# A row-sum kernel: the last two rows loaded in column pieces and shared by two engines, and the group stores moved from the POOL queue to the ACT queue

## The chip, the cores and the metric

The kernel runs on one core of one Trainium2 chip. The metric is the device time of one execution in microseconds (us), read on the chip. The profile of the kernel before is of a run that took 163.31 us.

Three words are used throughout. A load or store is *issued* when a queue (SP, ACT or POOL) hands it to the 16 DMA engines; it has *landed* when its semaphore is complete in the trace; its *packets* are the trace's records of what the DMA engines moved. The engines are VectorE (DVE in the profile), ScalarE (ACT), GpSimd (POOL) and SyncE (SP).

## The reference

```python
def setup_inputs():
    batch, seq, dim = 32, 512, 1024
    return {"x": np.random.randn(batch, seq, dim).astype(np.float32)}

def reference(x):
    return np.sum(x, axis=-1).astype(np.float32)
```

The kernel reads 67.11 MB, adds up 16384 rows of 1024 numbers, and writes 64 KB. There is next to nothing to compute; the loads set the time.

## The kernel before

Each of the 128 partitions gets 128 rows, in 8 groups of 16. Groups 0 to 6 are one 8 MB load each, into three rotating buffers. VectorE adds up all 16 rows of a tile in one instruction; in the seventh tile ScalarE takes half of the rows, with the accumulator of an ACTIVATE whose ordinary output nobody reads. The eighth group is loaded in shrinking parts (8, 4, 2, 1 rows), and its last row in three column pieces, so that little work is left when the last bytes arrive.

```python
        def vec(dst, src):
            nc.vector.tensor_reduce(
                out=dst, in_=src, axis=mybir.AxisListType.X, op=mybir.AluOpType.add
            )

        def act(dst, src, n):
            nc.scalar.activation(
                out=scratch[:, :n],                  # one SBUF tile, not read by anyone
                in_=src,
                func=mybir.ActivationFunctionType.Copy,
                accum_out=dst,
            )
        # ... rows_of(): one load, then vec() on the first rows and act() on the others
        def store(eng, g0, g1):
            eng.dma_start(
                out=out_v[:, g0:g1],
                in_=sums[:, g0 * BIG : g1 * BIG].rearrange("p (g j) -> p g j", j=BIG),
            )

        for i in range(nbig):                        # seven 8 MB tiles
            t = inpool.tile([P, BIG * dim + 2], fp32)
            rows_of(t, 0, BIG, i * BIG, BIG // 2 if i == nbig - 1 else 0)
            if i % 3 == 2:
                store(nc.gpsimd, i - 2, i + 1)       # group stores, POOL queue
        store(nc.gpsimd, nbig - 1, nbig)
        # ... parts of 8, 4 and 2 rows, shared by both engines; one whole row for ScalarE
        cuts = [0, 384, 768, dim]                    # the last row
        for c0, c1 in zip(cuts, cuts[1:]):
            nc.sync.dma_start(out=last[:, c0:c1], in_=rows_from(j, 1)[:, 0, c0:c1])
        for i, (c0, c1) in enumerate(zip(cuts, cuts[1:])):
            if c1 < dim:
                vec(last[:, dim + i : dim + i + 1], last[:, c0:c1])   # partial sums, beside the data
            else:
                vec(sums[:, j : j + 1], last[:, c0 : dim + i])        # 256 columns + 2 partial sums
        store(nc.sync, nbig, nbig + 1)
```

## Time and profile before

| | before |
|---|---|
| time, median of 3 runs | 162.79 us (162.73 to 162.85) |
| span of the profile | 161.5 us |
| load packets | 1.0 to 157.90 us |
| last piece landed | 158.37 us |
| last reduction | 158.68 to 159.10 us |
| final store | issued 159.17, landed 160.59 us |

First the page of the kernel before: busy time of each engine, the DMA line of the table by slices (tenths of busy time, 40 slices), the load queue with its share of 16 engines' span, and the chain that ended last by line.

```profile
span 161.5 us, 124 instructions
...
DVE 121.4 (75%) x13; ACT 19.7 (12%) x33; POOL 2.4 (1%) x7
...
DMA  8997998997997997996996996996997996999990
...
q1 hardware_dynamic: 2160, 67.12, 97.1%
...
DMA t<-in_x_dram 74%; DVE sums L66 22%; SPq L81 1%; DVE t L66 1%; DVEq L66 0%
```

The load queue fills 97.1% of the span and VectorE 75%, so the DMA stream is the bound. The 22% of VectorE in the chain is the time in which a later load waits in the queue for its buffer; the stream does not run dry meanwhile, because two more loads are under way. A steady 64 KB packet takes 2.418 us in the trace, so 16 engines move 16 x 65536 B / 2.418 us = 433.7 GB/s. The Trainium skill, "DMA: Bandwidth & Descriptors", Where 436 GB/s comes from, puts the ceiling of the ports at 435.2 GB/s, and the trace agrees. In the middle of this kernel next to nothing can be gained.

The end is another matter. This is the timeline of the kernel before (start, duration, engine, line, instruction; in brackets how long the engine sat idle before it and for what):

```profile
138.55 8.69 DVE L66 TENSOR_REDUCE sums<-t 128x8 f32<-128x8192 f32 x1 [2.15 <-DMA t<-in_x_dram]
...
157.09 1.06 ACT L71 ACTIVATE scratch<-t 128x1024 f32<-128x1024 f32 x1
157.64 1.01 DVE L66 TENSOR_REDUCE t<-t 128x1 f32<-128x384 f32 x2 [0.68 <-DMA t<-in_x_dram]
158.06 0.19 ACT L71 ACTIVATION_READ_ACCUMULATOR scratch<-t 128x1 f32 x1
158.68 0.42 DVE L66 TENSOR_REDUCE sums<-t 128x1 f32<-128x258 f32 x1
159.17 0.35 SPq L88 DMA_DIRECT2D out_dram<-sums  x1
```

The last piece has landed at 158.37, but VectorE is still on its two 384-column pieces (the "x2" line) until 158.66. So the last reduction starts 0.31 us after its data is there, and all of the final store and the closing barriers follow it.

### The profile page before, as it was taken

The page shows a single profiled execution, that of the slowest core. Times are in us where ns is not written, and L with a number is a line of the kernel's source. Part 1 is how long each engine was busy: PE and PEld are TensorE (multiplying, and loading weights), DVE is VectorE, ACT ScalarE, POOL GpSimd, SP SyncE. Part 2 cuts the span into 40 slices and gives each one's busy share as a digit, 9 for nine tenths or more (in the row PEclk, how much of TensorE's full clock was granted, in tenths as well). Part 3 has the DMA queues.
Part 4 walks back from the last instruction along what each step waited for, and adds up shares of the span by engine and source line. Part 5 has one row for each costly group of instructions (what it writes and reads, how often), then busy time and mean ns, then how long its engine had stood idle before and what let it go on. Part 6 is the DMA issues. An engine that isn't in the chain of part 4 may idle for free.

```text
span 161.5 us, 124 instructions
## 1 busy us (share of the span) xinstructions
DVE 121.4 (75%) x13; ACT 19.7 (12%) x33; POOL 2.4 (1%) x7
## 2 busy tenths in 40 slices
DVE  0000049998699968999499994999949997697883
ACT  3000000000000000000000000000000000698891
POOL 0000000000000000000200000000000001001000
DMA  8997998997997997996996996996997996999990
GB/s 260 519 438 341 519 406 373 519 438 341 519 454 325 519 471 308 519 487 292 519 493 293 519 487 292 519 487 292 519 454 325 519 487 292 391 491 389 410 392 14
DMA packets 2256, 67.18 MB, mean 416 GB/s; under 512 B 416, under 2 KB 848, under 8 KB 976
## 3 DMA queue, kind: packets, MB, share of 16 engines
q1 hardware_dynamic: 2160, 67.12, 97.1%
q0 software_dynamic: 96, 0.06, 0.1%
HBM read 67.11 MB, written 0.07 MB: 416 GB/s over the span
## 4 chain that ended last, share of the span: by engine, by line
DMA 74%; DVE 22%; SPq 1%; issue 0%; DVEq 0%
DMA t<-in_x_dram 74%; DVE sums L66 22%; SPq L81 1%; DVE t L66 1%; DVEq L66 0%
## 5 line engine op out<-in xcount | busy, mean ns | idle before, releaser
L66 DVE TENSOR_REDUCE sums<-t 128x16 f32<-128x16384 f32 (+5 forms) x11 | 120.4, 10941 | 37.1 <-DMA t<-in_x_dram 37.0
L71 ACT ACTIVATE scratch<-t 128x1024 f32<-128x1024 f32 x16 | 16.9, 1057 | 137.8 <-DMA t<-in_x_dram 137.3
L88 POOL DMA_DIRECT2D out_dram<-sums x3 | 2.2, 732 | 146.2 <-DVE sums L66 135.4
L71 ACT ACTIVATION_READ_ACCUMULATOR scratch<-t 128x1 f32 x16 | 3.0, 186 | 0.0
L66 DVE TENSOR_REDUCE t<-t 128x1 f32<-128x384 f32 x2 | 1.0, 549 | 0.7 <-DMA t<-in_x_dram 0.7
L71 ACT ACT_TABLE_LOAD x1 | 1.3, 1283 | 0.8 <-PEq L135 0.8
L135 POOL MEMSET const-float32-0.0<- 128x1 f32 x1 | 0.1, 98 | 0.2 <-issue 0.2
L135 POOL MEMSET const-bfloat16-1.0<- 128x1 bf16 x1 | 0.1, 101 | 0.0
L135 POOL MEMSET const-uint8-127<- 128x1 uint8 x1 | 0.1, 99 | 0.0
L135 POOL MEMSET const-float32-1.0<- 128x1 f32 x1 | 0.1, 98 | 0.0
## 6 DMA issues: line engine op xcount, KB each, us to landing
t<-in_x_dram SPq DMA_DIRECT2D x1, 4096.0 KB, 31.2
t<-in_x_dram SPq DMA_DIRECT2D x1, 2048.0 KB, 35.9
t<-in_x_dram SPq DMA_DIRECT2D x1, 1024.0 KB, 37.8
t<-in_x_dram SPq DMA_DIRECT2D x1, 512.0 KB, 38.6
t<-in_x_dram SPq DMA_DIRECT2D x2, 192.0 KB, 38.6
t<-in_x_dram SPq DMA_DIRECT2D x1, 128.0 KB, 38.4
t<-in_x_dram SPq DMA_DIRECT2D x7, 40.8
out_dram<-sums POOLq DMA_DIRECT2D x2, 24.0 KB, 7.9
```

The costliest lines, as they stand in the source:

```text
L66: nc.vector.tensor_reduce(out=dst, in_=src, axis=mybir.AxisListType.X, op=mybir.AluOpType.add)
L71: nc.scalar.activation(out=scratch[:, :n], in_=src, func=mybir.ActivationFunctionType.Copy, accum_out=dst,)
L81: nc.sync.dma_start(out=block, in_=rows_from(j, n))
L88: eng.dma_start(out=out_v[:, g0:g1], in_=sums[:, g0 * BIG : g1 * BIG].rearrange("p (g j) -> p g j", j=BIG),)
L135: nc = _bacc.Bacc("TRN2", target_bir_lowering=False, num_devices=1)
```

## The change

The intent has three parts: share the last two rows between VectorE and ScalarE, so that the last reduction does not queue behind VectorE's other pieces; take the group stores out of the load stream and make one ACT-queue store of them at the end; and let ScalarE write its unread output to PSUM, with four buffers. The diff, cut (`tc.manual_schedule()` came with the change):

```diff
-        tc.tile_pool(name="scratch", bufs=1) as spool,
+        tc.tile_pool(name="unread", bufs=4, space=bass.MemoryType.PSUM) as upool,
+        tc.manual_schedule(),
 ...
-            if i % 3 == 2:
-                store(nc.gpsimd, i - 2, i + 1)
-        store(nc.gpsimd, nbig - 1, nbig)
 ...
-        rows_of(t, a, 1, nbig * BIG + a, 1)          # and the last row in 384, 384, 256
+        for width in (640, 256, 128):                # two rows in each piece
+            if len(parts) == k:
+                at += k                              # room for row 0's partial sums
+            part = t[:, at : at + 2 * width].rearrange("p (n d) -> p n d", n=2)
+            nc.sync.dma_start(out=part, in_=rows_from(j, 2)[:, :, c : c + width])
+            ...
+        for i, part in enumerate(parts[:k]):
+            vec(w[:, i : i + 1], part[:, 0, :])                       # row 0: VectorE
+            act(w[:, k + 2 * width + i : ...], part[:, 1, :], pieces[i])  # row 1: ScalarE
+        store(nc.scalar, 0, last)                    # all seven group stores at once
+        vec(sums[:, j : j + 2], w.rearrange("p (n d) -> p n d", n=2)) # 2 x (128 + 2)
         store(nc.sync, last, last + 1)
```

The partial sums of row 0 stand just ahead of the last piece and those of row 1 just behind it, so one reduction over two runs of 130 finishes both rows. The order of instructions on VectorE is unchanged; on ScalarE the store comes after its second piece.

More of the change, by code (lines that the diff above doesn't have):

```diff
@@ L51, in rows_from @@
         return x_g[j // BIG, :, j % BIG : j % BIG + n, :]
-    nbig = J // BIG - 1
-    tail = [(8, 4), (4, 2), (2, 1)]
+    last = J // BIG - 1
+    pieces = (640, 256, 128)
     with (
         tc.tile_pool(name="in", bufs=3) as inpool,
-        tc.tile_pool(name="scratch", bufs=1) as spool,
+        tc.tile_pool(name="unread", bufs=4, space=bass.MemoryType.PSUM) as upool,
         tc.tile_pool(name="stage", bufs=1) as stpool,
+        tc.manual_schedule(),
     ):
         sums = stpool.tile([P, J], fp32)
-        scratch = spool.tile([P, dim], fp32)
         def vec(dst, src):
@@ L70, in act @@
         def act(dst, src, n):
+            unread = upool.tile([P, dim], fp32)
             nc.scalar.activation(
-                out=scratch[:, :n],
+                out=unread[:, :n],
                 in_=src,
@@ L76, in act, with rows @@
             )
-        def rows_of(t, a, n, j, n_act):
+        def rows(t, a, n, j, n_act):
             nv = n - n_act
@@ L81, in rows_of @@
             nc.sync.dma_start(out=block, in_=rows_from(j, n))
-            if nv:
-                vec(sums[:, j : j + nv], block[:, :nv, :])
+            vec(sums[:, j : j + nv], block[:, :nv, :])
             for q in range(nv, n):
@@ L91, in store @@
             )
-        for i in range(nbig):
-            t = inpool.tile([P, BIG * dim + 2], fp32)
-            rows_of(t, 0, BIG, i * BIG, BIG // 2 if i == nbig - 1 else 0)
-            if i % 3 == 2:
-                store(nc.gpsimd, i - 2, i + 1)
-        store(nc.gpsimd, nbig - 1, nbig)
-        t = inpool.tile([P, BIG * dim + 2], fp32)
+        for g in range(last):
+            t = inpool.tile([P, BIG * dim + 4], fp32)
+            rows(t, 0, BIG, g * BIG, BIG // 2 if g == last - 1 else 0)
+        t = inpool.tile([P, BIG * dim + 4], fp32)
         a = 0
-        for n, n_act in tail:
-            rows_of(t, a, n, nbig * BIG + a, n_act)
+        j = last * BIG
+        for n in (8, 4, 2):
+            rows(t, a, n, j + a, n // 2)
             a += n
-        rows_of(t, a, 1, nbig * BIG + a, 1)
-        a += 1
-        j = nbig * BIG + a
-        last = t[:, a * dim :]
-        cuts = [0, 384, 768, dim]
-        for c0, c1 in zip(cuts, cuts[1:]):
-            nc.sync.dma_start(out=last[:, c0:c1], in_=rows_from(j, 1)[:, 0, c0:c1])
-        for i, (c0, c1) in enumerate(zip(cuts, cuts[1:])):
-            if c1 < dim:
-                vec(last[:, dim + i : dim + i + 1], last[:, c0:c1])
-            else:
-                vec(sums[:, j : j + 1], last[:, c0 : dim + i])
-        store(nc.sync, nbig, nbig + 1)
+        j += a
+        at = a * dim
+        k = len(pieces) - 1
+        parts = []
+        c = 0
+        for width in pieces:
+            if len(parts) == k:
+                at += k
+            part = t[:, at : at + 2 * width].rearrange("p (n d) -> p n d", n=2)
+            nc.sync.dma_start(out=part, in_=rows_from(j, 2)[:, :, c : c + width])
+            parts.append(part)
+            at += 2 * width
+            c += width
+        w = t[:, at - 2 * width - k : at + k]
+        for i, part in enumerate(parts[:k]):
+            vec(w[:, i : i + 1], part[:, 0, :])
+            act(w[:, k + 2 * width + i : k + 2 * width + i + 1], part[:, 1, :], pieces[i])
+        store(nc.scalar, 0, last)
+        vec(sums[:, j : j + 2], w.rearrange("p (n d) -> p n d", n=2))
+        store(nc.sync, last, last + 1)
 _INS = ['x']
```

## The prediction

> What bounds the kernel now. The DMA stream. The chain of waits gives 74% of the span to loads and its last 38.6 us are the load queue; the table by slices shows DMA near full until the last slice, and the queue table puts the load queue's packets at 97.1% of 16 engines' span. In the packet records, load packets run from 1.0 us to 157.90 us of a 161.5 us span. VectorE is 75% busy and ScalarE 12%: both have slack until the last two rows. So only three things can move the time: work added to or taken from the DMA stream, the stretch from last landing to the final reduction, and the stores after it.
>
> The tail before. The last piece's semaphore is complete at 158.37, but VectorE runs three short reductions in a row (384, 384, 258 elements: 0.55, 0.54, 0.42 us) and starts the last at 158.68, ending 159.10. The final store is issued at 159.17, its packets move 160.01 to 160.22, it has landed at 160.59, and 0.9 us of closing barriers follow.
>
> What the change does.
> 1. Stream, removed: three POOL stores. Their packets cost each DMA engine two 65 ns, one 27 ns and three 9 ns records, about 0.18 us, all before the stream's end.
> 2. Stream, added: the last two rows now come in runs of 2560, 1024 and 512 bytes. The records give 159 ns for 4096 B, 66 for 1536, 46 for 1024 and 27 for 512, so I estimate 103 for 2560. Per engine: 16 x (103+46.5+27) = 2.82 us against 8 x 159 + 16 x 66 + 8 x 46.5 = 2.70 us. Net about +0.1 us; with 1, the last landing moves about 0.1 us earlier, to 158.3.
> 3. Last reduction. Estimated landings 157.1, 157.85, 158.3. VectorE (about 1.05 ns an element plus 0.14 us) does 640 and 256 elements by 158.4. ScalarE takes 1057 ns for 1024 elements today; the Trainium skill, "ScalarE: Activation LUTs", What ACT_TABLE_LOAD costs, gives 0.833 ns an element, which leaves 0.2 us fixed. This trace has one length only and cannot confirm the slope. With the 0.09 us by which the accumulator read outlasts it, ScalarE finishes its two pieces near 158.6. So the last reduction (two rows of 130, 0.42 us) starts at about 158.65 and ends at 159.05: one wait, VectorE's own queue, is exchanged for another, ScalarE's. Gain 0 to 0.15 us. ScalarE's output in PSUM may take a little off each ACTIVATE.
> 4. Moved into the tail: one ACT-queue store of 896 runs of 64 B. Its wait is long satisfied, so it issues right after ScalarE's second piece is dispatched, about 158.1. At 11 ns a run (the final store's records) it costs each engine 56 x 11 = 0.6 us. If it starts 0.84 us after issue, as the final store does, it is done by about 159.9, before the final store's packets at 160. Little slack: if generating 896 runs is slower, it delays the final store or lands last.
>
> Everything before 155 us should stay as it was. Sum: 0.1 to 0.3 us gained, against a possible 0 to 1 us lost to the ACT store.
>
> Predicted 162.7 us, range 162.0 to 163.7; faster by over 2%: 2%; within 2%: 94%; slower by over 2%: 4%.
>
> Right if: the last landing is within 0.2 us of 158.3; the last VectorE reduction is released by ScalarE and ends 158.9 to 159.2; ACT-queue packets end before the final store's start. Wrong if: the ACT store's packets run past 160.1, or the final store's first packet comes later than 0.85 us after issue; or the stream ends earlier by over 0.3 us, which would mean that the POOL stores cost loads more than their own packets; or fixed launch cost outside the span changes as POOL's queue falls idle.

## The result, and the profile after

| | before | after |
|---|---|---|
| time, median of 4 runs | 162.82 us (162.73 to 163.11) | 162.98 us (162.72 to 163.11) |
| ratio | | 1.0005 (95% interval 0.9987 to 1.0022) |
| span of the profile | 161.5 us | 161.2 us |

A ratio is the mean time of one kernel's fast runs over that of the other's in the same rounds, so it is not quite the ratio of the medians.

The page of the kernel after, the same lines and the new queue q10, which is the ACT store:

```profile
span 161.2 us, 123 instructions
...
DVE 121.5 (75%) x13; ACT 18.5 (12%) x35; POOL 0.2 (0%) x4
...
DMA  8996996996996996996996996996996996998992
...
q1 hardware_dynamic: 2400, 67.12, 97.3%
q10 hardware_dynamic: 912, 0.06, 0.3%
...
DMA t<-in_x_dram 75%; DVE sums L67 22%; SPq L83 1%; DVE t L67 1%; ACTq L89 0%; ACT unread L73 0%; DVEq L67 0%
```

The timeline of the kernel after:

```profile
138.14 8.69 DVE L67 TENSOR_REDUCE sums<-t 128x8 f32<-128x8192 f32 x1 [2.32 <-DMA t<-in_x_dram]
...
157.09 1.14 DVE L67 TENSOR_REDUCE t<-t 128x1 f32<-128x640 f32 x2 [0.54 <-DMA t<-in_x_dram]
157.15 0.71 ACT L73 ACTIVATE unread<-t 128x640 f32<-128x640 f32 x1 [0.61 <-DMA t<-in_x_dram]
157.79 0.19 ACT L73 ACTIVATION_READ_ACCUMULATOR unread<-t 128x1 f32 x1
157.88 0.37 ACT L73 ACTIVATE unread<-t 128x256 f32<-128x256 f32 x1
157.94 0.41 ACTq L89 DMA_DIRECT2D out_dram<-sums  x1
158.19 0.19 ACT L73 ACTIVATION_READ_ACCUMULATOR unread<-t 128x1 f32 x1
158.41 0.42 DVE L67 TENSOR_REDUCE sums<-t 128x2 f32<-128x260 f32 x1 [0.18 <-ACT unread L73]
158.86 0.36 SPq L89 DMA_DIRECT2D out_dram<-sums  x1
```

VectorE now has a gap before the last reduction, "[0.18 <-ACT unread L73]": the wait that ends last changed its owner, as intended. But the last piece landed at 158.12, so the last reduction still starts 0.29 us after its data: VectorE is on its second piece until 158.23, 0.11 us, and then waits 0.18 us for ScalarE. The ACT store is issued under ScalarE's last ACTIVATE; its packets run from 158.90 to 159.63, and the final store's first packet follows at 159.72.

The span is 0.3 us shorter while the time is not. The two traces differ before the change has done anything: the first load landed at 22.39 before and at 21.69 after, mostly because the first round of 64 KB packets took 3.57 us on average in one profile (the slowest 3.98) and 3.11 us in the other (3.36), with the same code at the start. The whole span is therefore a poor measure of a change this small. Counting from the landing of the last 8 MB tile removes that. The table below is worked out from semaphore, instruction and packet records of each trace; it has the experiments too, which come next. "Closing" is from the final store's landing to the end of the span.

| trace | last piece landed, us after the last 8 MB tile | last reduction starts, us after that piece | it ends, us after the tile | closing, us | end of span, us after the tile |
|---|---|---|---|---|---|
| before | 19.85 | 0.31 | 20.58 | 0.95 | 23.01 |
| before_again | 19.85 | 0.32 | 20.59 | 0.94 | 23.00 |
| after | 20.00 | 0.29 | 20.72 | 0.88 | 23.05 |
| a_repeat (after) | 19.92 | 0.30 | 20.65 | 0.88 | 22.98 |
| b_pieces_pool | 20.00 | 0.30 | 20.72 | 1.01 | 23.20 |
| c_store_only | 19.77 | 0.31 | 20.50 | 0.82 | 22.80 |
| c_again | 19.85 | 0.34 | 20.60 | 0.81 | 22.89 |
| d_scratch_sbuf | 19.93 | 0.45 | 20.80 | 0.88 | 23.14 |
| f_store_early | 20.08 | 0.17 | 20.67 | 0.88 | 23.01 |
| g_no_cut | 19.68 | 0.02 | 21.99 | 1.01 | 24.51 |
| h_cut_even | 19.96 | 0.15 | 20.67 | 0.88 | 23.01 |

Two traces of the same kernel differ by 0.01 to 0.10 us in the last column, against up to 0.2 us in the span. In that column before is 23.01 and after 23.02 (means of two): no difference.

### The profile page after: what moved, and what is told of

The parts are those of the page before. It is cut to its first block, busy times and chain, and to the rows that moved or that the text cites. A ratio compares the mean times of both kernels' runs of the same rounds, so it can differ in the third digit from the quotient of the medians.

```text
span 161.2 us, 123 instructions
## 1 busy us (share of the span) xinstructions
DVE 121.5 (75%) x13; ACT 18.5 (12%) x35; POOL 0.2 (0%) x4
## 4 chain that ended last, share of the span: by engine, by line
DMA 75%; DVE 22%; SPq 1%; issue 0%; ACTq 0%; ACT 0%; DVEq 0%
DMA t<-in_x_dram 75%; DVE sums L67 22%; SPq L83 1%; DVE t L67 1%; ACTq L89 0%; ACT unread L73 0%; DVEq L67 0%
## 5 line engine op out<-in xcount | busy, mean ns | idle before, releaser
L73 ACT ACTIVATE unread<-t 128x1024 f32<-128x1024 f32 (+2 forms) x17 | 16.3, 956 | 139.0 <-DMA t<-in_x_dram 139.0
L73 ACT ACTIVATION_READ_ACCUMULATOR unread<-t 128x1 f32 x17 | 3.2, 188 | 0.0
L67 DVE TENSOR_REDUCE t<-t 128x1 f32<-128x640 f32 (+1 forms) x2 | 1.1, 614 | 0.5 <-DMA t<-in_x_dram 0.5
```

The source lines that it names most:

```text
L67: nc.vector.tensor_reduce(out=dst, in_=src, axis=mybir.AxisListType.X, op=mybir.AluOpType.add)
L73: nc.scalar.activation(out=unread[:, :n], in_=src, func=mybir.ActivationFunctionType.Copy, accum_out=dst,)
```

## The experiments

Twelve kernels ran, in three sets of four, each set on one chip beside runs of the kernel before; all gave correct results. Times are medians.

### a_repeat: the changed kernel again, as a control

No edit.

> The changed kernel once more, unaltered, as a control. Main theory (the change gives and takes about 0.1 to 0.3 us at the end of a load stream that sets the time): 0.998 to 1.002 of the kernel before, and the first round of 64 KB load packets, which took 2.9 to 3.4 us here against 3.3 to 4.0 us in the profile before (a steady one takes 2.42 us), lands anywhere in that range again, because the code of the start is the same. The 0.7 us by which the first load landed earlier would then be chance. Rival 1 (the 0.3 us shorter span of the profile is the change's own gain): the first load lands at 21.7 again and the ratio is at or below 0.998.

Measured: 162.97 us, ratio 0.9999 (0.9980 to 1.0018). The first load landed at 21.86. The expectation that the first round of packets may lie anywhere in the old range held weakly: it took 2.7 to 3.5 us (in the first profile of before single packets took 2.9 to 4.0). What matters more is the ratio: no gain.

### before_again: the kernel before again

No edit.

> The kernel before once more, for its profile alone. Its first load landed at 22.39 in the profile before; in the nine profiles of other kernels, all with the same code at the start, it landed between 21.69 and 21.92. Main theory (the 0.3 us shorter span of the changed kernel's profile is mostly this, and it is chance): the first load lands near 21.8 now, the span is about 161.0, and counted from the landing of the last full tile (138.5 before) the last piece again lands 19.8 to 19.9 us later and the last reduction ends 20.55 to 20.65 us later. Rival (the slow start belongs to the kernel before): 22.3 to 22.5 again.

Measured: 163.07 us, ratio 1.0000 (0.9976 to 1.0024). The first load landed at 21.82, the first round of packets took 3.07 us on average, and the last reduction ended 20.59 us after the last tile, the same as in the first profile to 0.01 us. The span was 161.3, not 161.0, because slow packets, most of them between 95 and 125 us, took 0.36 us of the better start back (116.50 us from the first landing to that of the last 8 MB tile, against 116.14). So the slow start does not belong to the kernel before, and the tail is repeatable.

### b_pieces_pool: the column pieces without the store move

```diff
             rows(t, 0, BIG, g * BIG, BIG // 2 if g == last - 1 else 0)
+            if g % 3 == 2:
+                store(nc.gpsimd, g - 2, g + 1)
+        store(nc.gpsimd, last - 1, last)
 ...
-        store(nc.scalar, 0, last)
```

> The column pieces and the PSUM output alone: the group stores go back to the POOL queue, in the stream. Main theory: the stores' packets cost each DMA engine 0.18 us before the last landing, and the ACT store was off the critical path, so 0.1 to 0.2 us longer than the changed kernel (0.1%), 1.000 to 1.002 of before; from the landing of the last full tile to that of the last piece about 0.1 us more than the 20.0 us of the changed kernel. Rival (the ACT store costs the tail 0.3 us or more): shorter than the changed kernel by 0.2 us or more, ratio 0.998 or less.

Measured: 163.25 us, ratio 1.0014 (0.9997 to 1.0030); in the trace the end comes 23.20 us after the tile, 0.19 us after that of before. The last piece landed 20.00 us after the tile, as in the changed kernel and not 0.1 us later. So the pieces alone cost about 0.19 us in the trace (0.15 in the landing, 0.06 in the closing), and the store move gives about that back; but not where it was expected, in the stream: 0.13 us of it is in the closing, 1.01 us here against 0.88 in the changed kernel. The rival, that the ACT store is what costs, fell.

### c_store_only and c_again: the store move without the pieces

```diff
# the kernel before, plus manual_schedule()
-            if i % 3 == 2:
-                store(nc.gpsimd, i - 2, i + 1)
-        store(nc.gpsimd, nbig - 1, nbig)
 ...
             else:
+                store(nc.scalar, 0, nbig)
                 vec(sums[:, j : j + 1], last[:, c0 : dim + i])
```

> The store move alone, on the tail of before (one row whole, then 384, 384, 256 columns). ScalarE has no work after its last row, so the ACT queue issues the store near 157.2, and its packets (0.7 us in the changed kernel) move from about 158.0, after the last load packet. Main theory: no cost in the tail and 0.18 us less in the stream: 0.998 to 1.000 of before; the last reduction still waits for VectorE's own queue and ends about 0.7 us after the last landing. Rival (the ACT store disturbs the last loads or the final store): the final store's landing comes more than 1.5 us after its issue, ratio 1.002 or more.

> The store move alone once more, because its first ratio, 0.9976 (0.9962 to 0.9990, about 0.39 us), is twice what its trace shows: counted from the landing of the last full 8 MB tile, its final store landed 21.98 us later against 22.07 before, and one POOL store (0.07 us) lies ahead of that point. Main theory: the store move is worth 0.15 to 0.2 us, ratio 0.9985 to 0.9995 on average over both sets of runs, and the rest of the first ratio was the scatter of the start. Rival (the POOL stores cost the loads twice what their packets show, or something outside the trace): 0.9976 again.

Measured: first 162.76 us, ratio 0.9976 (0.9962 to 0.9990); again, on another chip, 163.10 us, ratio 1.0001 (0.9980 to 1.0023). The two disagree, and each is scatter around something small. The traces are steadier: the end comes 22.80 and 22.89 us after the tile, 0.16 us before that of before on average. The tail of the first c trace:

```profile
137.94 8.69 DVE L67 TENSOR_REDUCE sums<-t 128x8 f32<-128x8192 f32 x1 [2.13 <-DMA t<-in_x_dram]
...
156.45 0.41 ACTq L89 DMA_DIRECT2D out_dram<-sums  x1
156.94 1.03 DVE L67 TENSOR_REDUCE t<-t 128x1 f32<-128x384 f32 x2 [0.68 <-DMA t<-in_x_dram]
158.00 0.42 DVE L67 TENSOR_REDUCE sums<-t 128x1 f32<-128x258 f32 x1
158.49 0.35 SPq L89 DMA_DIRECT2D out_dram<-sums  x1
```

The ACT store is issued 1.5 us before VectorE's last reduction and is in nobody's way. This is the version that the traces put ahead of both kernels, by 0.16 us or 0.1%. The times don't settle it: one interval excludes 1 and the other sits on it.

The 0.16 us has two parts. The closing is 0.12 us shorter. With POOL's queue idle, GpSimd's closing drain takes 70 to 75 ns in place of 93 to 101 and its clearing of semaphores 92 to 93 in place of 136 (0.07 us, in the changed kernel as well); most of the rest is one wait instruction of SyncE fewer, some 60 ns, behind the final landing (one here, two in before and in the changed kernel, three in b_pieces_pool). The other part is in the stream, 0 to 0.08 us in the two traces, less than the 0.11 us of packet records of two POOL stores that lie behind that tile. The remaining POOL store, the first in time, lies ahead of it and is seen by itself: in the first profile of before and in b_pieces_pool the load around it landed 19.39 and 19.41 us after the one before, against 19.36 in the kernel after, so 0.04 to 0.06 us for 0.074 us of records. In before_again it is 19.48; but d_scratch_sbuf and k_half_runs, without a POOL store, have 19.44 and 19.72 there, so the scatter of slow packets can do as much.

### d_scratch_sbuf: ScalarE's unread output in SBUF again

```diff
-        tc.tile_pool(name="unread", bufs=4, space=bass.MemoryType.PSUM) as upool,
+        tc.tile_pool(name="unread", bufs=1) as upool,
```

(and the tile is made once, as in the kernel before)

> The changed kernel with ScalarE's unread output back in one SBUF tile. ScalarE is the last releaser of the final reduction in the changed kernel. Main theory: back-to-back ACTIVATEs go back from 1.04 to 1.18 us apart, so the second piece begins about 0.14 us later and the final reduction starts about 0.45 us after the last landing in place of 0.29: 0.15 us longer, 0.1%. Rival (PSUM or SBUF makes no difference at this place): the final reduction starts 0.29 us after the last landing again.

Measured: 163.05 us, ratio 1.0005 (0.9986 to 1.0023): the time can't tell. The trace can: the last reduction starts 0.45 us after the last landing, as expected, against 0.29. The groups of ScalarE by shape (busy us, mean ns), with PSUM in the kernel after:

```profile
L73 ACT ACTIVATE unread<-t 128x640 f32<-128x640 f32 x1 | 0.7, 707 | 0.6 <-DMA t<-in_x_dram 0.6
L73 ACT ACTIVATE unread<-t 128x256 f32<-128x256 f32 x1 | 0.4, 368 | 0.0
```

and with SBUF in d_scratch_sbuf:

```profile
L73 ACT ACTIVATE unread<-t 128x640 f32<-128x640 f32 x1 | 0.7, 737 | 0.6 <-DMA t<-in_x_dram 0.6
L73 ACT ACTIVATE unread<-t 128x256 f32<-128x256 f32 x1 | 0.4, 416 | 0.0
```

An ACTIVATE into PSUM is 30 to 48 ns shorter. The rest of the 0.16 us is a later start: the second piece starts 0.86 us after the first, against 0.73. With one buffer an ACTIVATE may have to wait for the one before it, but place and number of buffers were changed together here, so which of the two does it is not shown. The Trainium skill, "ScalarE: Activation LUTs", Step-by-step, says that an ACTIVATE to PSUM is faster than one to SBUF; the runs agree. They agree as well with the 0.833 ns an element of its section What ACT_TABLE_LOAD costs: in SBUF, (737 - 416) / 384 = 0.836 ns. In PSUM the same two instructions give (707 - 368) / 384 = 0.88.

### h_cut_even: other cuts

```diff
-    pieces = (640, 256, 128)
+    pieces = (512, 320, 192)
```

> The changed kernel with cuts at 512, 320 and 192 columns in place of 640, 256 and 128, so that both engines are done with their first two pieces sooner and the last reduction waits less. Main theory: last landing about 0.03 us earlier (longer runs), ScalarE done about 0.05 to 0.1 us after it in place of 0.26, but the last reduction grows from 0.42 to 0.55 us: a gain of 0 to 0.1 us, not to be seen in the time; ratio 0.999 to 1.001. Rival (the wait for ScalarE is worth its full 0.18 us): the reduction ends 0.2 us earlier, counted from the last landing, than the 0.71 us of the changed kernel.

Measured: 162.76 us, ratio 0.9984 (0.9969 to 0.9999). In the trace the wait did shrink, from 0.29 to 0.15 us, and the last reduction grew from 0.42 to 0.56 us: it ends 20.67 us after the tile, against 20.72 and 20.65. The gain was handed over, not kept. The small ratio has no counterpart in the trace and is taken for scatter, as the first one of c.

### g_no_cut: no pieces at all

```diff
-    pieces = (640, 256, 128)
+    pieces = (1024,)
```

One load for both rows and one VectorE reduction over both.

> The changed kernel with its last two rows as one load and one VectorE reduction over both, to size what cutting is worth at all. Main theory: last landing 0.1 us earlier than in the changed kernel (runs of 4096 bytes), then one reduction of 2048 elements (2.29 us in this trace) in place of 0.29 us of waiting and 0.42 of reduction: it ends about 1.5 us later, ratio 1.008 to 1.010. Rival (the end of the kernel is set by the ACT store, not by this chain): ratio under 1.004.

Measured: 164.27 us, ratio 1.0079 (1.0054 to 1.0104).

```profile
157.60 2.29 DVE L67 TENSOR_REDUCE sums<-t 128x2 f32<-128x2048 f32 x1 [1.36 <-DMA t<-in_x_dram]
159.96 0.35 SPq L89 DMA_DIRECT2D out_dram<-sums  x1
```

So cutting the end is worth 1.3 us; both kernels have that already, in two forms. The last landing came at 19.68 us after the tile, which is 0.25 us earlier than the usual 19.93 of the cut kernels, not the 0.1 us expected, because the two whole rows of a partition lie together and come as one run of 8192 bytes. (The edit also moved the ACT store: with no piece left for ScalarE it was issued at 155.18, and part of its packets, 156.55 to 157.50, ran among the last load packets.) This is the closest sight of what short runs cost: 8 packets of 312 ns for each engine make 2.50 us, the 48 packets of the pieces 2.82 us.

### k_half_runs: shorter runs still (did not test what it was meant to)

```diff
-            nc.sync.dma_start(out=part, in_=rows_from(j, 2)[:, :, c : c + width])
+            half = width // 2
+            for h in (0, half):
+                nc.sync.dma_start(out=part[:, :, h : h + half],
+                                  in_=rows_from(j, 2)[:, :, c + h : c + h + half])
```

> The changed kernel with each of its three pieces loaded as two loads of half the columns, so runs of 1280, 512 and 256 bytes; the reductions stay as they are. Main theory: a run costs about 8 ns beside its bytes on a DMA engine, so 48 more runs and three more semaphore writes lengthen the stream by about 0.4 us: last landing 20.35 to 20.45 us after the last full tile in place of 20.0, ratio 1.002 to 1.003. That would be the sign that the shorter runs are why the column pieces land 0.1 us later than the tail before. Rival (run length is free in a full stream): last landing still 20.0 us after.

Measured: 165.94 us, ratio 1.0172 (1.0141 to 1.0202), verdict "unclear" against the 2% line; six times what was expected or more, and for another reason. The chain that ended last (start, duration, what):

```profile
118.45 38.04 DMA t<-in_x_dram
156.49 0.02 issue
156.51 0.37 SPq L119
156.88 0.04 issue
156.92 0.47 SPq L119
157.39 0.04 issue
157.44 3.32 DMA t<-in_x_dram
```

SyncE issued the last five piece loads only from 156.51 on. The trace says what the first of these five, the second half of the first piece, waited for: the semaphore of the load issued just before it, the first half of the same piece, which landed at 156.49. (The two-row part had landed at 155.64, and the other semaphores that these loads reuse had been complete for 8 us or more.) Why the build puts that wait there was not looked into; the two halves lie interleaved in the tile. The stream ran dry: no load bytes moved between 156 and 157 us. The experiment says nothing about run length; it does say that cutting a load can break how far ahead loads are issued. g_no_cut stands in for it.

### e_store_quarters and l_store_by_groups: how much room the ACT store has

```diff
# e_store_quarters
-        store(nc.scalar, 0, last)
+        for q in range(0, BIG, 4):
+            nc.scalar.dma_start(out=out_v[:, 0:last, q : q + 4],
+                in_=sums[:, : last * BIG].rearrange("p (g j) -> p g j", j=BIG)[:, :, q : q + 4])
# l_store_by_groups
-        store(nc.scalar, 0, last)
+        for g in range(0, last, 2):
+            store(nc.scalar, g, min(g + 2, last))
```

> The changed kernel with its ACT store cut into four stores of four columns each, so 3584 runs of 16 bytes in place of 896 of 64. The ACT store of the changed kernel landed 0.23 us before the final store. Main theory: a run costs each DMA engine about as long whatever its few bytes (8 to 11 ns), so the packets take about 2.2 us from 158.9 on, the last of the four lands near 161.5, that wait ends last, and the time grows by about 1 us: ratio about 1.006. Rival (the store is free in the tail, with room to spare): ratio within 0.002 of 1.

> The changed kernel with its ACT store cut by groups into four stores (2, 2, 2 and 1 groups), with the runs left at 64 bytes, to tell why the four column quarters took 4.3 us and not 1. Theory A (16-byte runs are slow to be acknowledged: there the packets ended at 161.3 but the landing came at 164.4): no such delay here, the packets end about 160.3 and the last landing follows 0.4 us later, near 160.7, ratio 1.002 to 1.004. Theory B (four stores in flight on one queue are slow, whatever their runs): landing after 163, ratio over 1.015.

Measured: e_store_quarters 167.46 us, ratio 1.0267 (1.0245 to 1.0289), slower; l_store_by_groups 163.50 us, ratio 1.0035 (1.0009 to 1.0062). The waits of SyncE's queue on the stores at the end (total us, times, longest), first of e_store_quarters, then of l_store_by_groups, then of the kernel after:

```profile
SPq L157 <- DMA out_dram<-sums: 5.2, 2, 3.3
```

```profile
SPq L154 <- DMA out_dram<-sums: 1.6, 2, 1.4
```

```profile
SPq L153 <- DMA out_dram<-sums: 0.9, 2, 0.8
```

Both show that the ACT store is near the edge: make it longer and it ends the kernel. The size of e was missed by four. Its packets ended at 161.27, within 0.3 us of the estimate (7 ns for 16 bytes), but the last store landed only at 164.39, 3.1 us after its last packet. With 64-byte runs, also four stores, the last packet ended at 160.51 and the landing came at 160.88, 0.4 us later and 0.2 us later than expected. So the delay belongs to the 16-byte runs, not to the number of stores (theory A). Nor is it the number of runs, of which e has four times as many: its first quarter alone has 896, as the changed kernel's store has, and landed at 161.06, 1.72 us after its last packet, where the changed kernel's store took 0.42 us. The Trainium skill, "DMA: Bandwidth & Descriptors", Anatomy of one DMA, puts most of a transfer's fixed cost (told there for the GpSimd path) in the write receipt of the target memory; the gap between last packet and landing fits that, but no run here looks inside it.

### f_store_early: the ACT store in the stream

```diff
             rows(t, 0, BIG, g * BIG, BIG // 2 if g == last - 1 else 0)
+        store(nc.scalar, 0, last)
 ...
-        store(nc.scalar, 0, last)
```

> The changed kernel with the same ACT store issued earlier, right after ScalarE's rows of the last full tile (near 147.5), so that its 896 packets run among the load packets. Main theory: the stream is the bound, so its 0.5 to 0.6 us of packets for each engine are paid in full: the last piece lands 20.5 us after the last full tile in place of 20.0, and the ratio rises to 1.002 to 1.004. Rival (64-byte packets slip in beside the loads for nothing): last landing still 20.0 us, ratio within 0.001 of the changed kernel.

Measured: 163.07 us, ratio 1.0002 (0.9986 to 1.0019). The main theory's 0.5 to 0.6 us did not come: the last piece landed 20.08 us after the tile, against the usual 19.92 to 20.00.

```profile
138.32 8.69 DVE L67 TENSOR_REDUCE sums<-t 128x8 f32<-128x8192 f32 x1 [2.36 <-DMA t<-in_x_dram]
...
147.09 0.42 ACTq L89 DMA_DIRECT2D out_dram<-sums  x1
...
158.55 0.42 DVE L67 TENSOR_REDUCE sums<-t 128x2 f32<-128x260 f32 x1 [0.18 <-ACT unread L73]
```

The store's packets lie between 150.89 and 157.86, 11 ns each, so 56 x 11 = 0.6 us of records for each engine, spread out among the load packets. The Trainium skill, same page, Queues, rings and completion order, says that an engine takes turns between its queues packet by packet, and the spread agrees: from 152 to 154 us, among load records of 8 KB and 309 ns, 13 to 14 store records on average start in each quarter of a microsecond, about one for each load record (16 x 0.25 / 0.309 = 13). The page's packet holds several descriptors, though, while the turns here go by single records of the trace.

The landing came only 0.08 to 0.16 us later than in the two traces of the kernel after, about a quarter of the records' sum at most. The last load packet moved more: it ended 19.74 us after the tile, against 19.47 and 19.40, about 0.3 us or half of the sum; the landing then followed it by 0.34 us in place of 0.52. All records between the tile and that packet sum to 19.96 us for each engine in a stretch of 19.74, so 0.2 us of them at least overlap: their sum is not stream time. The rule "what enters a full stream is paid in full" does not hold here for small stores (one trace).

## Why the prediction was right, point by point

The time lay where it was predicted, 162.98 us against 162.7 (162.0 to 163.7), and "within 2%" was right. That says little for the reasons: the range is 1.7 us wide, and the parts argued about are 0.1 to 0.3 us. The reasons hold to a different degree.

1. *The stream is the bound, and only three things at its ends can move the time.* Right. Every kernel here follows its last landing, except where a store (e, l) or the issue of loads (k) was made to end last.
2. *Stream, added: about 0.1 us for shorter runs.* Right, if a little small: the last piece lands 0.11 us later after the last tile (19.96 against 19.85, means of two), although two POOL stores fewer lie in between. Between kernels with the same stores it is 0.15 us: 20.00 in b_pieces_pool against 19.85 before, 19.96 after against 19.81 in the two traces of c. g_no_cut shows the same cost from the other side, 0.25 us for dropping them all.
3. *Stream, removed: 0.18 us for the POOL stores.* Half right. The first store cost 0.04 to 0.06 us, near its records. But behind the last tile the records of two of the three stores are 0.11 us, and c_store_only and c_again landed only 0 to 0.08 us earlier than before, and b_pieces_pool, which puts the stores back, landed as the changed kernel does. As f_store_early showed, such records need not be stream time. The step is mis-sized; what made up for it was not foreseen: the closing barriers are 0.07 us shorter, 0.88 against 0.94. So the net of points 2 and 3 went the wrong way: a landing 0.1 us earlier, at 158.3, was forecast. It came at 158.12, within the 0.2 us that the prediction allowed, but by luck: this trace was already 0.40 us ahead when the last 8 MB tile landed (138.12 against 138.52). Counted from the tile, 158.3 is 19.78, and 20.00 and 19.92 were measured.
4. *One wait is exchanged for another.* Right, and this is the heart of it: 0.31 us of VectorE's queue became 0.29 us, of which ScalarE's wait ends last (0.11 us of VectorE's second piece, then 0.18 us for ScalarE). The last reduction was put at 158.65 to 159.05 and ran from 158.41 to 158.83. That is outside the 158.9 to 159.2 which the prediction named as a sign of being right; counted from the tile it ended later than forecast, 20.72 against 20.53. The gain of 0 to 0.15 us did not come: counted from the last tile, the reduction ends 0.1 us later than before (20.72 and 20.65 against 20.58), since the later landing outweighs the 0.02 us. h_cut_even shows that other cuts move the wait into the last reduction. PSUM, of which "a little" was expected, was worth 0.16 us together with its four buffers, 0.45 against 0.29 in d_scratch_sbuf; without it the pieces would have lost more.
5. *The ACT store ends before the final store starts, with little slack.* Right: 159.63 against 159.72. (The final store's first packet came 0.858 us after its issue, just over the 0.85 that the prediction named as a sign of being wrong; b_pieces_pool, which has no ACT store, has 0.853, so the ACT store is not behind it.) It landed at 160.06, 0.23 us before the final store; e_store_quarters and l_store_by_groups show that more would have been paid.
6. *The predicted sum of 0.1 to 0.3 us gained* did not come; the central 162.7 leaned on it. In the traces the parts cancel: the store move gives 0.16 us (two profiles of c) and the pieces take about 0.19 us (one profile of b); each is little more than the 0.1 us by which two traces of one kernel can differ.

What stays open: single parts of 0.1% are below what the times resolve (c gave 0.9976 on one chip and 1.0001 on another), so that c_store_only is faster than both kernels rests on the tails of two traces. Why the first round of packets varies from run to run, and why slow packets appear in the middle of some traces, was not looked into.

## What to carry to other kernels

When a stream is at its ceiling, re-cutting the last pieces mostly moves the same few tenths of a microsecond between the landing, the wait for the slower engine and the last instruction; ask which of the three grows before expecting a gain. Compare ends from a landmark late in the trace, not from the start of the span, when the start itself scatters by more than the change. And take the sum of small packets' records as an upper limit of what a store costs a full stream, and keep stores' runs from getting very short when their landing is the last thing waited for.

## What the Trainium skill lacked or had wrong

- "DMA: Bandwidth & Descriptors" says that transfers below 512 bytes are read-modify-write, but not what very short runs do to the landing of a store: with 16-byte runs the last landing came 3.1 us after the last packet (1.7 us for the first 896 runs alone), with 64-byte runs 0.4 us after it.
- The same page describes packet-by-packet turns between queues, but gives no figure for how far small store packets overlap with load packets: 0.6 us of 64-byte records for each engine put off the last load packet of a full stream by about 0.3 us and its landing by 0.08 to 0.16 us.
- The same page does not mention the slow first round of a stream: 64 KB packets took 3.0 to 3.6 us on average (fourteen traces) against 2.42 us later on, and the first landing lay between 21.69 and 22.39 us.
- No page that was looked up has the closing cost of a used POOL queue: GpSimd's closing drain took 93 to 101 ns in place of 70 to 75 and its semaphore clearing 136 in place of 92 to 93.
